# Half of a block's in-projection by Strassen products, with the weight sums made on the spot

## The chip, the cores and the metric

The kernel runs on one core of a Trainium2 chip. The metric is the time of one execution on the device in microseconds (us), lower is better. The engines of the core are PE (TensorE, matmuls), DVE (VectorE), ACT (ScalarE), POOL (GpSimd) and SP (SyncE). In this kernel SP issues the loads and POOL the stores; ACT and DVE evict, convert and add.

## What is computed

The reference is a trunk of two layers over 2048 tokens of width 1024. Per layer:

```python
shift, scale, gate = split(silu(c) @ w_ada[l] + b_ada[l])
h = rms_norm(x, g_pre[l]) * (1 + scale) + shift
u_a, b_a, c_a, gate_a, u_p, gate_p = split(h @ w_in[l])      # 6 x 512 columns
y_a = b_a * causal_conv3(c_a * u_a, w_conv[l]) * silu(gate_a)
y_p = pool_windows(u_p, w_pool[l], pool_scale[l]) * silu(gate_p)
y = concat(y_a, y_p) @ w_out[l]
x = x + gate * rms_norm(y, g_post[l])
```

Everything is fp32. The two large products of a layer are the in-projection (1024 by 3072 weights) and the out-projection (1024 by 1024).

## The kernel before

**Tiling.** Tokens lie along the free dimension, features on the 128 partitions. The work falls into four blocks (l, b): layer 0 with tokens 0 to 1023 and 1024 to 2047, then layer 1 with the same; they are called blocks 0 to 3. A block is an in-projection and an out-projection. Each fp32 product is made from three passes in the reduced type fp32r: every operand is split into a high half (a cast by ACT, L209 and L739) and a low half (operand less high half, by DVE, L219 and L749), and the passes are high by high, high by low, low by high (`PASSES`). One matmul is 128x128 weights by 512 tokens.

**In-projections.** Blocks 0 and 1 use `in_phase`: 24 column groups (kinds ua, up, ca, gp, ba, ga; four of each), 8 steps of k, 3 passes, 2 halves of tokens, so 1152 matmuls in block 1. Blocks 2 and 3 use `in_seven`: the groups are taken in 12 pairs (`PAIRS`: P is up and gp, A is ua and ca, B is ba and ga), and each pair is computed by the seven products of Strassen's scheme in Winograd's form, 12 matmuls each: 1008 in all. The scheme needs four sums of the pair's weight quarters, S1 to S4, and four of the operand's, T1 to T4. The weight sums of layer 1 are made by background tasks in blocks 0 and 1 (`sum_task`), split, stored to DRAM (`sums`) and loaded by POOL in blocks 2 and 3 (L724). The operand sums are made in the out-projection before (`operands` in `out_phase`).

**Order.** The order of each engine is written out by hand: DVE, ACT, PE, POOL and SP each run the instructions in the order of the code. Work that follows a group (evictions, gate, windows, convolution) is queued and given out in small steps between the matmuls. `Paced` spreads background tasks evenly over the turns of an in-projection; a task has a load that is issued when the task before it starts, and steps. The tasks are: `finish_tasks` (fin: an out-projection's result times the norm ry, plus x, stored as the next x; L1095 to L1115), `ada_task` (products of the conditioning, L265), `mix_task` (small matmuls on the pool weights of layer 1, tiles wupt and ps_wu, L419) and `sum_task` (L462 to L479). In block 1 the tasks are eight mixes, 16 fins, 16 adas of two products each, and the sums of the P pairs; the others were made in block 0. Weights are loaded, and their halves made, two to three halves ahead of their use.

**Tiles.** `working(t, r, n, w, v)` sets the number of buffers of each ring: `tmp` (1024 tokens wide), `half` (512), `landing` (512, loads of background tasks), raw weights, and v. A ring hands its tiles out in turn; who takes a tile waits until the last user of that tile is done. Block 1 has working(8, 6, 4, 3, 0), and there a wide sum task takes one tile of `tmp` for its four inputs (raw01).

**Between the phases.** An out-projection is 8 groups of 48 matmuls, `OUT_ORDER` giving the order of k for the first group (k = 3 last). At the end of a Strassen block the last steps of y and the first out-projection weights are made by the functions of `closing`.

## Time and profile before

| | us |
|---|---|
| median of 3 runs | 1411.99 |
| least, greatest | 1409.59, 1415.24 |
| profiled execution | 1412.32 |
| its span in the trace | 1410.5 |
| PE busy | 1385.0 |
| DVE busy | 920.7 |
| ACT busy | 493.5 |
| block 1: in-projection, out-projection (PE) | 393.6 to 666.6, to 753.8 |
| blocks 2 and 3: in-projections (PE) | 753.8 to 984.2, 1071 to 1301.8 |

The profiled execution has its own time, and the span of its trace is a little shorter than that time, since it runs from the first to the last instruction. "Busy" adds up the durations of an engine's instructions. A row of the timeline merges equal instructions that follow each other.

### The profile page before, as it was taken

Reading aid. Unit: us, or ns where it says so; the run is one execution under the profiler, and the core shown is the slowest. Engines: PE = TensorE matmul, PEld = TensorE weight load, DVE = VectorE, ACT = ScalarE, POOL = GpSimd, SP = SyncE. Lnnn points to the kernel's source line nnn. Section 1 sums busy time; section 2 is a strip of 40 time slices with the busy share of each in tenths; the row PEclk is TensorE's granted clock in tenths of the full one; section 3 lists DMA queues with packets and bytes.
Section 4 is the critical chain, followed back from the end, with each engine's and each line's share of the span. In section 5 each row is a group of like instructions: output and inputs, shape, how many; then the busy total and the mean of one; then the engine's idle time right before and its main releaser. Section 6 shows DMA issues by size and latency. Waiting matters only on the chain.

```text
span 1410.5 us, 17844 instructions
## 1 busy us (share of the span) xinstructions
PE 1385.0 (98%) x6250; PEld 1140.9 (81%) x6250; DVE 920.7 (65%) x1540; ACT 493.5 (35%) x862; POOL 219.7 (16%) x350
## 2 busy tenths in 40 slices
PE   8999999999999999999999999999999999999996
PEld 4778888888887888888888888888887888888796
DVE  7764778754545585866766776768866665657455
ACT  5332334345443323233546122123646121113421
POOL 0001232311101111101112222110112222211000
PEclk9999999999999999999999999999999999999998
DMA  8506777734436655645559888888459777877422
GB/s 323 179 31 205 232 250 273 247 130 156 157 116 200 228 180 193 227 161 172 183 187 310 259 246 260 264 246 259 175 188 311 224 225 221 244 226 245 144 90 90
DMA packets 143115, 291.22 MB, mean 206 GB/s; under 512 B 15921, under 2 KB 32305, under 8 KB 143026
## 3 DMA queue, kind: packets, MB, share of 16 engines
q1 hardware_dynamic: 96338, 171.58, 37.4%
q0 software_dynamic: 46688, 118.51, 25.5%
q8 instruction: 49, 0.80, 0.2%
q14 instruction: 40, 0.33, 0.1%
HBM read 217.67 MB, written 72.35 MB: 206 GB/s over the span
## 4 chain that ended last, share of the span: by engine, by line
PE 93%; DMA 3%; DVE 2%; issue 1%; ACT 1%; POOL 0%; SPq 0%; ACTq 0%; DVEq 0%; POOLq 0%
PE ps_in L393 36%; PE ps_in L817 29%; PE ps_out L393 24%; PE ps_wu L419 1%; DMA ws<-sums 1%; DMA yt<-fin 1%; DMA wupt<-wupt 1%; PE ps_warm L1219 1%; PE ps_stat L1236 1%; PE ps_stat L311 0%; DMA raw<-wout 0%; DVE y L186 0%; PE ps_c L1283 0%; DVE win L495 0%; DMA yraw<-yin 0%
## 5 line engine op out<-in xcount | busy, mean ns | idle before, releaser
L817 PE MATMUL ps_in<-h,ws 128*128 128x512 f32 x2016 | 458.6, 389 | 0.7 <-DMA ws<-sums 0.7
L393 PE MATMUL ps_in<-h,ws 128*128 128x512 f32 x1968 | 450.6, 390 | 0.0
L817 PEld LDWEIGHTS ps_in<-h,ws 128*128 128x128 f32 x2016 | 378.1, 188 | 80.2 <-DMA ws<-sums 1.6
L393 PEld LDWEIGHTS ps_in<-h,ws 128*128 128x128 f32 x1968 | 368.5, 188 | 76.2
L393 PE MATMUL ps_out<-y,ws 128*128 128x512 f32 (+1 forms) x1728 | 354.8, 367 | 2.6 <-DVE y L186 2.6
L393 PEld LDWEIGHTS ps_out<-y,ws 128*128 128x128 f32 x1728 | 299.9, 189 | 56.9 <-DVE y L186 2.9
L209 ACT CAST ws<-raw 128x512 fp32r<-128x512 f32 x146 | 89.9, 622 | 301.3 <-PE ps_in L393 156.7
L219 DVE TENSOR_TENSOR ws<-raw,ws 128x512 fp32r<-128x512 f32 x146 | 99.8, 688 | 125.3 <-ACT ws L209 125.1
L724 POOL DMA_DIRECT2D ws<-sums x96 | 67.7, 706 | 205.5 <-PE ps_in L817 182.6
L393 PE MATMUL ps_in<-h,w 128*128 128x512 f32 x336 | 81.9, 402 | 5.2 <-DVE h L385 2.8
L393 PEld LDWEIGHTS ps_in<-h,w 128*128 128x128 f32 x336 | 63.6, 191 | 22.6 <-DVE h L385 3.6
L739 ACT CAST ws<-raw 128x512 fp32r<-128x512 f32 x72 | 43.2, 617 | 66.8 <-PE ps_in L817 37.0
L1004 POOL DMA_DIRECT2D ysp<-yg x48 | 26.2, 545 | 241.6 <-ACT yg L1003 241.4
L265 DVE SCALAR_TENSOR_TENSOR adaw<-adaw,cb 128x512 f32<-128x512 f32 x64 | 43.1, 686 | 11.3 <-DMA adaw<-wada 9.6
L749 DVE TENSOR_TENSOR ws<-raw,ws 128x512 fp32r<-128x512 f32 x72 | 49.3, 684 | 0.0
L1012 DVE TENSOR_TENSOR acc<-acc,sq 128x512 f32<-128x512 f32 x42 | 28.9, 692 | 27.0 <-ACT sq L1009 27.0
L859 ACT ACTIVATE second<-second 128x1024 f32<-128x1024 f32 x16 | 17.0, 1061 | 82.6 <-DVE second L853 79.8
L838 ACT COPY v<-ps_in 128x512 f32<-128x512 f32 x24 | 14.1, 588 | 84.7 <-PE ps_in L817 84.7
L476 POOL DMA_DIRECT2D sums<-s13h x24 | 17.7, 739 | 146.6 <-ACT s13h L468 97.7
L1099 DVE TENSOR_TENSOR fin<-fin,ry 128x512 f32<-128x512 f32 x48 | 32.9, 685 | 8.3 <-DMA fin<-ysp 8.3
L853 DVE TENSOR_TENSOR second<-ps_in,v 128x512 f32<-128x512 f32 x16 | 11.0, 690 | 41.3 <-PE ps_in L817 41.3
L1003 ACT ACTIVATE yg<-ps_out,gg 128x512 f32<-128x512 f32 x48 | 33.1, 689 | 11.9 <-PE ps_out L393 11.9
(172 smaller groups left out, 1258.4 us busy)
## 6 DMA issues: line engine op xcount, KB each, us to landing
ws<-sums POOLq DMA_DIRECT2D x96, 512.0 KB, 7.6
raw<-win SPq DMA_DIRECT2D x122, 256.0 KB, 4.6
adaw<-wada SPq DMA_DIRECT2D x64, 256.0 KB, 4.8
raw<-wout SPq DMA_DIRECT2D x64, 256.0 KB, 3.2
sums<-raw POOLq DMA_DIRECT2D x48, 256.0 KB, 5.4
ysp<-yg POOLq DMA_DIRECT2D x48, 256.0 KB, 3.7
fin<-ysp SPq DMA_DIRECT2D x48, 256.0 KB, 4.3
raw<-win SPq DMA_DIRECT2D x80, 128.0 KB, 4.7
```

Of the source, the lines that this page charges most:

```text
L209: nc.scalar.copy(self.ws[m][:, 0], self.raws[m].rearrange("p (a b) -> p a b", b=P))
L219: nc.vector.tensor_tensor(t[:, 1], raw, t[:, 0].bitcast(F32), op=ALU.subtract)
L265: nc.vector.scalar_tensor_tensor(w[n], w[n], 1.0, cb[:, n * HS : (n + 1) * HS], op0=ALU.mult, op1=ALU.mult, accum_out=m[:, l, j : j + 1])
L393: nc.tensor.matmul(ps[s], lhsT=ws[k // KH][:, wi, k % KH, :], rhs=rhs(k, ri, s), start=first and (wi, ri) == PASSES[0], stop=last and (wi, ...
L724: nc.gpsimd.dma_start(ops[m].rearrange("p a b c -> p a (b c)"), sums[l, n][:, :, SUM[a]])
L739: nc.scalar.copy(ops[m][:, 0], raws[m].rearrange("p (a b) -> p a b", b=P))
L749: nc.vector.tensor_tensor(ops[m][:, 1], raw, ops[m][:, 0].bitcast(F32), op=ALU.subtract)
L817: nc.tensor.matmul(ps, lhsT=ops[m][:, wi, k, :], rhs=h[hn][k][:, ri, :], start=p < 4 and k == 0 and (wi, ri) == (0, 0), stop=k == KH - 1 a ...
L1003: nc.scalar.activation(t, ps[s], AF.Copy, scale=gg[:, l, j : j + 1])
L1004: nc.gpsimd.dma_start(ysp[l, b][:, j, s * HS : (s + 1) * HS], t)
L1012: tt(accs[s], accs[s], q, op=ALU.add)
L1099: nc.vector.tensor_tensor(e[0], e[0], ry[l, b, s], op=ALU.mult)
```

## The change

In block 1 the groups with index below `PLAIN` = 2 (12 of 24) stay plain, and the other 12 are computed as six Strassen pairs. Their weight sums don't come from DRAM: the class `Sevenths` loads the four quarters of a pair, and `add` makes S1, S2, S3 (L758 to L760 of the changed kernel) and later S4 (L765) on DVE; all seven weight operands are then split into high (ACT) and low half (DVE, L787). The out-projection of block 0 makes plain operands and, of the same values, the four differences (`both_operands`); what the Strassen half needs later is stored to `late4` and loaded as 16 background tasks (`fills`) in the plain half. The products y of block 1 go to DRAM and back as in blocks 2 and 3. The 16 conditioning tasks of layer 1 move from block 1 into block 0. The sum tasks of block 1 become narrow (wide=False): they take two tiles of `landing` (raw0, raw1) in place of one of `tmp`; three run in the plain half and five in the Strassen half, with six and ten fins. Block 1 has working(5, 6, 5, 6, 2). Three background tasks are primed and not one. The last product's evictions in every Strassen block stand behind the last closing function, not ahead of it. Where helpers moved, the changed kernel's numbers are L476 for L474 (a sum task's low halves), L1180, L1181 and L1186 for L1095, L1096 and L1101 (a fin's two loads and its sum), L868 for L817 (Strassen's matmuls) and L897 and L901 for L844 and L848 (evictions).

```diff
+    late4 = dram.tile([P, KH, 2, TB], F32, name="late4")
...
         def put_y(k, t, o, n):
+            if some:
+                nc.gpsimd.dma_start(yin[l, b][:, k, o : o + n], t)
+                return
...
-        bg.prime(1)
+        bg.prime(3)
...
+    class Sevenths:
+
+        def __init__(self, l, ring, pairs, made=False):
+            self.l, self.ring, self.pairs, self.made = l, ring, pairs, made
...
+                elif q == 0:
+                    self.raws[m] = self.raws[m + 1] = self.quarter(n, 0, 0)
+                    self.raws[m + 2] = self.quarter(n, 1, 0)
+                    self.raws[m + 5] = self.quarter(n, 1, 1)
+                elif q == 4:
+                    self.raws[m] = self.raws[m + 2] = self.quarter(n, 0, 1)
+                self.loaded += 1
+        def add(self, m):
+            tt = nc.vector.tensor_tensor
+            if m % 7 == 1:
+                self.low(m)
+                r11, r21, r22 = self.raws[m], self.raws[m + 1], self.raws[m + 4]
+                s1 = self.raws[m + 2] = half("s1")
+                tt(s1, r21, r22, op=ALU.add)
+                tt(r21, r11, r21, op=ALU.subtract)
+                tt(r11, s1, r11, op=ALU.subtract)
+                self.s2 = r11
+                return 3 * E2
+            if m % 7 == 6:
+                self.low(m - 1)
+                tt(self.raws[m], self.raws[m], self.s2, op=ALU.subtract)
+                return E2
+            return 0
+        def high(self, upto):
+            self.load(upto)
+            us = 0
+            while self.highs < min(upto, self.nm):
+                m = self.highs
+                if m in self.raws:
+                    if self.made:
+                        us += self.add(m)
+                    nc.scalar.copy(self.place(m)[:, 0], self.raws[m].rearrange("p (a b) -> p a b", b=P))
+                self.highs += 1
+            return us
+        def low(self, upto):
+            us = 0
+            while self.settled < min(upto, self.nm):
+                m = self.settled
+                if m in self.raws:
+                    t, raw = self.ops[m], self.raws.pop(m).rearrange("p (a b) -> p a b", b=P)
+                    nc.vector.tensor_tensor(t[:, 1], raw, t[:, 0].bitcast(F32), op=ALU.subtract)
+                    us += E2
+                self.settled += 1
+            return us
+        def settle(self, upto):
+            return self.high(upto) + self.low(upto)
...
+                if final and p == 6:
+                    closing[p](kept)
...
-                if at == 6:
-                    closing[at](kept)
-                if (n or p > 5) and n < len(PAIRS) - 1 and at != -1:
+                if (n or p > 5 or not opening) and n < len(pairs) - 1 and at != -1:
...
+        def both_operands(k):
             xs = []
 
             def load():
-                xs.append(tmp("xin")[:, :TB])
-                nc.sync.dma_start(xs[0], x_src(nl, k, nb * TB, TB))
+                for kk in (k, k + KH):
+                    xs.append(tmp("xin")[:, :TB])
+                    nc.sync.dma_start(xs[-1], x_src(nl, kk, nb * TB, TB))
 
             def steps():
-                t = xs[0]
-                nc.vector.scalar_tensor_tensor(t, t, apre[:, nl, k : k + 1], rn, op0=ALU.mult, op1=ALU.mult)
-                yield E1
+                a, c = xs
+                for t, kk in ((a, k), (c, k + KH)):
+                    nc.vector.scalar_tensor_tensor(t, t, apre[:, nl, kk : kk + 1], rn, op0=ALU.mult, op1=ALU.mult)
+                    yield E1
                 yield None
                 parts = []
-                for s in range(NH):
-                    hp0[s][k] = slot(next(hp), [P, 2, HS], "h")
-                    u = t[:, s * HS : (s + 1) * HS]
-                    parts.append((hp0[s][k], u))
-                    nc.scalar.activation(hp0[s][k][:, 0], u, AF.Identity, bias=mod[:, nl, k : k + 1])
+                for t, kk in ((a, k), (c, k + KH)):
+                    nc.scalar.activation(t, t, AF.Identity, bias=mod[:, nl, kk : kk + 1])
+                    for s in range(NH):
+                        d = hp0[s][kk] = slot(hplaces[8 * s + kk], [P, 2, HS], "h")
+                        u = t[:, s * HS : (s + 1) * HS]
+                        nc.scalar.copy(d[:, 0], u)
+                        parts.append((d, u))
                 yield None
                 for d, u in parts:
-                    prenorm_lo(d[:, 0], d[:, 1], nl, k, u)
+                    tt(d[:, 1], u, d[:, 0].bitcast(F32), op=ALU.subtract)
                     yield E2
+                a0, a1, c0, c1 = [u for _, u in parts]
+                for dst, p, m in ((a0, a1, a0), (a1, c1, a1), (c1, c1, a0), (c0, c0, c1)):
+                    tt(dst, p, m, op=ALU.subtract)
+                    yield E2
+                nc.gpsimd.dma_start(spill4[:, k, 0], a)
+                nc.gpsimd.dma_start(spill4[:, k, 1], c)
...
+                if both and j == KT - 1 and n == 6:
+                    nxt.high(3)
+                    nxt.settle(2)
+                if not both and j == KT - 1 and n == 4:
+                    nxt.load(2)
...
+            rest += [ada_task(1, j) for j in list(range(8, 16)) + list(range(8))]
+            rest += [call_task(lambda: (ada_fin(1, 1, 0, KT), ada_fin(1, 0, 0, KT)), 0.5)]
...
+    with working(5, 6, 5, 6, 2), tc.manual_schedule():
+        plain = [(kind, i) for kind, i in IN_ORDER if i < PLAIN]
+        pairs = [(kind, i) for kind, i in PAIRS if i >= PLAIN]
+        first = in_weights(0, plain, 0, turned(ws.places, 16))
+        h, fills, opening, hrhs = out_phase(0, 0, y, 0, 1, ws, hplaces, yorder, first, True)
+        ring = first.places + hplaces[8 : 8 + KH]
+        wts = Sevenths(0, ring, pairs, True)
         later = Later()
         mixes = [mix_task(1, g, n, later) for g in range(NCG) for n in range(2)]
         fins = finish_tasks(0, 0, later)
-        adas = [ada_task(1, j) for j in list(range(8, 16)) + list(range(8))]
-        adas += [call_task(lambda: (ada_fin(1, 1, 0, KT), ada_fin(1, 0, 0, KT)), 0.5)]
-        sums_ = [sum_task(1, n, u, True) for n, u in mine("P")]
-        tasks = between(mixes, fins[:4]) + between(between(adas, sums_), fins[4:])
-        ws = out_weights(0, first.places)
-        y = in_phase(0, 1, hrhs, tasks, later, None, yplaces, first.places, ws, first, opening)
-    wplaces = first.places
+        sums_ = [sum_task(1, n, u, False) for n, u in mine("P")]
+        cut = 6
+        tasks = between(fills, mixes) + between(fins[:cut], sums_[:3])
+        in_phase(0, 1, hrhs, tasks, later, None, None, first.places, wts, first, opening, plain)
+        hp = {}
+        for k in range(KH):
+            hp["B11", k], hp["B21", k], hp["B22", k] = hplaces[k], hplaces[KH + k], hplaces[12 + k]
+        it = iter(yorder)
+        for name in ("T2", "T3", "T1", "T4"):
+            for k in range(KH):
+                hp[name, k] = next(it)
+        ws, closing, done = block_end(0, 1, hp, ring, pairs, False, (3, 2, 3, 2, 2, 2))
+        kept = in_seven(0, 1, h, [], None, between(fins[cut:], sums_[3:]), later, wts, closing, pairs)
+        y, yorder, wplaces, hplaces, _ = done(kept)
```

**PE, in-projection of block 1.** ps_in are the sums of the in-projection, ps_wu those of a mix, ps_stat a mean of squares. Before, and changed:

```order
L419 MATMUL ps_wu<-wp,wupt 128x128 x4
L393 MATMUL ps_in<-h,ws 128x512 x366
L311 MATMUL ps_stat<-ah,ones 128x512
L311 MATMUL ps_stat<-al,ones 128x512
L393 MATMUL ps_in<-h,ws 128x512 x558
```

```order
L421 MATMUL ps_wu<-wp,wupt 128x128 x4
L395 MATMUL ps_in<-h,ws 128x512 x318
L868 MATMUL ps_in<-h,ws 128x512 x156
L313 MATMUL ps_stat<-ah,ones 128x512
L313 MATMUL ps_stat<-al,ones 128x512
L868 MATMUL ps_in<-h,ws 128x512 x312
```

Where 366 and 558 plain matmuls stood behind the last mix, 318 plain ones stand and then 468 of Strassen products (L868), around the first small statistics.

**DVE, second half of block 1's in-projection, at the end of a sum task.** s13 and s13h are a sum task's S1 and S3, raw01 or raw0 and raw1 its quarters, ws a weight's two halves, fin a finish task's tiles, ps_in an eviction. Before, and changed:

```order
L472 TENSOR_TENSOR s13_4870<-s13_4870,s13h_4871 128x512
L474 TENSOR_TENSOR raw01_4817<-raw01_4817 128x256 x2
L219 TENSOR_TENSOR ws_4941<-raw_4855,ws_4941 128x512
L604 TENSOR_TENSOR cv_4674<-cv_4674,sga_4945 128x1024
L265 SCALAR_TENSOR_TENSOR adaw_4898,mod_76<-adaw_4898,cb_70 128x512
L551 TENSOR_TENSOR y_4962<-cv_4674,y_4962 128x512
L551 TENSOR_TENSOR y_4964<-cv_4674,y_4964 128x512
L265 SCALAR_TENSOR_TENSOR adaw_4900,mod2_77<-adaw_4900,cb_70 128x512
L265 SCALAR_TENSOR_TENSOR adaw_4967,mod_76<-adaw_4967,cb_70 128x512
L219 TENSOR_TENSOR ws_4986<-raw_4896,ws_4986 128x512
L1115 TENSOR_TENSOR xacc_4450<-xacc_4450,fin_4866 128x512
L265 SCALAR_TENSOR_TENSOR adaw_4969,mod2_77<-adaw_4969,cb_70 128x512
```

```order
L474 TENSOR_TENSOR s13_4868<-s13_4868,s13h_4869 128x512
L476 TENSOR_TENSOR raw0_4812<-raw0_4812 128x256
L476 TENSOR_TENSOR raw1_4815<-raw1_4815 128x256
L787 TENSOR_TENSOR ws_4964<-raw_4841,ws_4964 128x512
L901 TENSOR_TENSOR second_4895<-ps_in_4974,second_4895 128x512
L1184 TENSOR_TENSOR fin_4916<-fin_4916,ry_3532 128x512
L1186 TENSOR_TENSOR fin_4917<-fin_4917,fin_4916 128x512
L787 TENSOR_TENSOR ws_4988<-raw_4921,ws_4988 128x512
L758 TENSOR_TENSOR s1_5013<-raw_4923,raw_4925 128x512
L759 TENSOR_TENSOR raw_4923<-raw_4921,raw_4923 128x512
L760 TENSOR_TENSOR raw_4921<-s1_5013,raw_4921 128x512
L1200 TENSOR_TENSOR xacc_4811<-xacc_4811,fin_4864 128x512
```

Before, a sum task's last low halves are followed by a weight's low half, the gate product and conditioning products, with the next fin eleven rows behind; now a fin's two steps stand three and four rows behind, then the low half and the sums of the next pair's weights.

**SP, the loads of the same stretch.** Each row is one load in the order of SP's queue; wu is the mixed pool weight, ysp the out-projection's stored result. Before, and changed:

```order
L200 DMA raw_4813<-win 128x512
L454 DMA raw01_4817<-win 128x256
L454 DMA raw01_4817<-wu1_2_94 128x256
L454 DMA raw01_4817<-win 128x256
L454 DMA raw01_4817<-wu1_2_94 128x256
L200 DMA raw_4855<-wu0_3_91 128x512
L1095 DMA fin_4866<-ysp0_0_130 128x512
L1096 DMA fin_4867<-xt 128x512
L200 DMA raw_4896<-wu0_3_91 128x512
L261 DMA adaw_4898<-wada 128x512
L261 DMA adaw_4900<-wada 128x512
L200 DMA raw_4943<-win 128x512
```

```order
L456 DMA raw0_4812<-win 128x256
L456 DMA raw0_4812<-wu1_2_94 128x256
L456 DMA raw1_4815<-win 128x256
L456 DMA raw1_4815<-wu1_2_94 128x256
L729 DMA raw_4841<-win 128x512
L1180 DMA fin_4864<-ysp0_0_131 128x512
L1181 DMA fin_4865<-xt 128x512
L1180 DMA fin_4916<-ysp0_0_131 128x512
L1181 DMA fin_4917<-xt 128x512
L729 DMA raw_4921<-wu0_3_91 128x512
L729 DMA raw_4923<-win 128x512
L729 DMA raw_4925<-win 128x512
```

Before, a sum task takes one tile of `tmp` (raw01) and the fin takes two of `landing`; now raw0, raw1 and four fin tiles are taken one after the other from `landing`, and the three quarters of the next pair stand behind the last of them.

## Rows read from the trace of the kernel before

**Rows 1.** Chain that ended last, by engine and line, share of the span.

```profile
PE 93%; DMA 3%; DVE 2%; issue 1%; ACT 1%; POOL 0%; SPq 0%; ACTq 0%; DVEq 0%; POOLq 0%
PE ps_in L393 36%; PE ps_in L817 29%; PE ps_out L393 24%; PE ps_wu L419 1%; DMA ws<-sums 1%; DMA yt<-fin 1%; DMA wupt<-wupt 1%; PE ps_warm L1219 1%; PE ps_stat L1236 1%; PE ps_stat L311 0%; DMA raw<-wout 0%; DVE y L186 0%; PE ps_c L1283 0%; DVE win L495 0%; DMA yraw<-yin 0%
```

**Rows 2.** What PE waited for, whole span: us in total, times, longest us.

```profile
PE ps_wu L419 <- DMA wupt<-wupt: 3.6, 2, 2.3
PE ps_out L393 <- DVE y L186: 2.6, 1, 2.6
```

**Rows 3.** Timeline of PE, merged: start us, us, line, operation, tiles, count.

```profile
535.47 126.70 PE L393 MATMUL ps_in<-h,ws 128*128 128x512 f32 x558
666.61 87.20 PE L393 MATMUL ps_out<-y,ws 128*128 128x512 f32 x384
765.57 117.17 PE L817 MATMUL ps_in<-h,ws 128*128 128x512 f32 x516
```

**Rows 4.** Stretches, length, busy us of PE, PEld, DVE, ACT, POOL; granted clock, DMA.

```profile
113.00:306.60 193.60, 192.35 (x873) 159.92 (x871) 133.28 (x264) 71.23 (x142) 48.80 (x70) 1.00 0.70 237
306.60:393.60 87.00, 87.00 (x385) 72.07 (x384) 45.96 (x61) 42.02 (x71) 7.60 (x14) 1.00 0.43 148
393.60:535.60 142.00, 139.67 (x648) 116.44 (x648) 82.58 (x148) 47.49 (x85) 18.32 (x30) 1.00 0.59 190
535.60:666.80 131.20, 131.20 (x580) 108.55 (x579) 87.33 (x162) 38.20 (x73) 19.05 (x28) 1.00 0.57 188
1310.00:1315.00 5.00, 5.00 (x16) 3.91 (x17) 2.38 (x4) 3.32 (x6) 0.00 (x0) 0.66 0.38 114
```

**Rows 5.** Timeline of DVE in block 2, and at the last in-projection's end.

```profile
797.13 1.28 DVE L514 SCALAR_TENSOR_TENSOR cv<-z,vecs,cv 128x1024 f32<-128x1024 f32 x1
798.33 0.69 DVE L1101 TENSOR_TENSOR fin<-fin 128x512 f32<-128x512 f32 x1
...
1306.45 0.68 DVE L873 TENSOR_TENSOR v<-ps_in,v 128x512 f32<-128x512 f32 x1
1307.17 0.69 DVE L773 TENSOR_TENSOR cv<-v,cv 128x512 f32<-128x512 f32 x1
1307.90 0.69 DVE L776 TENSOR_TENSOR cv<-cv,second 128x512 f32<-128x512 f32 x1
1308.51 0.69 DVE L219 TENSOR_TENSOR ws<-raw,ws 128x512 fp32r<-128x512 f32 x1
1309.11 1.29 DVE L186 TENSOR_TENSOR y<-cv,y 128x512 fp32r<-128x512 f32 x2
```

**Rows 6.** Lines by form, block 1's in-projection: busy us, mean ns.

```profile
L219 DVE TENSOR_TENSOR ws<-raw,ws 128x512 fp32r<-128x512 f32 x48 | 33.0, 687 | 38.5 <-ACT ws L209 38.5
L209 ACT CAST ws<-raw 128x512 fp32r<-128x512 f32 x48 | 29.9, 623 | 157.2 <-PE ps_in L393 99.7 <-issue 51.6 <-DMA raw<-wu 4.1
...
L474 DVE TENSOR_TENSOR raw<-raw 128x256 fp32r<-128x256 f32 x16 | 6.0, 417 | 0.0
L477 POOL DMA_DIRECT2D sums<-s x8 | 5.8, 728 | 15.4 <-DVE s L472 13.1 <-DMA fin<-ysp 2.1
L510 DVE TENSOR_SCALAR cv<-z,vecs 128x1024 f32<-128x1024 f32 x4 | 3.0, 748 | 0.0
```

**Rows 7.** DMA issues, second half of block 1, then first: us to landing.

```profile
sums<-raw POOLq DMA_DIRECT2D x10, 256.0 KB, 4.4
fin<-ysp SPq DMA_DIRECT2D x7, 256.0 KB, 3.3
fin<-xt SPq DMA_DIRECT2D x7, 256.0 KB, 4.1
sums<-s13h POOLq DMA_DIRECT2D x5, 256.0 KB, 2.7
...
sums<-raw POOLq DMA_DIRECT2D x6, 256.0 KB, 5.6
```

**Rows 8.** SP's waits in block 2's in-projection: us, times, longest.

```profile
SPq L1095 <- DMA x<-fin: 30.3, 5, 8.9
```

More of the change, by code (lines that the diff above doesn't have):

```diff
@@ L627, in in_phase @@
         else:
-            order, first = IN_ORDER, 0
+            order, first = some or IN_ORDER, 0
         for part in (range(0, 3), range(3, first)) if started else ():
@@ L673, in in_phase @@
                 turn = KT * (n - first) + k
+                if n == len(order) - 1 and k == 2:
+                    nxt.load(1)
                 if n == len(order) - 1 and k > KH:
@@ L704, in trunk, with place, quarter, load @@
     LOAD, HIGH, SETTLE = 6, 4, 3
-    def in_seven(l, b, h, fills, opening, tasks, later, ring, closing):
-        ops, raws = {}, {}
+    class Sevenths:
+        def __init__(self, l, ring, pairs, made=False):
+            self.l, self.ring, self.pairs, self.made = l, ring, pairs, made
+            self.ops, self.raws = {}, {}
+            self.nm = 7 * len(pairs)
+            self.loaded = self.highs = self.settled = 0
+        def place(self, m):
+            self.ops[m] = slot(self.ring[m % len(self.ring)], [P, 2, KH, P], "ws")
+            return self.ops[m]
+        def quarter(self, n, row, part):
+            kind, i = self.pairs[n]
+            t = held["w"].tile([P, HS], F32, tag="w", name="raw")
+            nc.sync.dma_start(t.rearrange("p (a b) -> p a b", b=P), w_src(self.l, PAIR_OF[kind][row], i, part))
+            return t
+        def load(self, upto):
+            while self.loaded < min(upto, self.nm):
+                m = self.loaded
+                n, q = divmod(m, 7)
+                a = PRODUCTS[q][0]
+                if a in SUM and not self.made:
+                    kind, i = self.pairs[n]
+                    t = self.place(m)
+                    nc.gpsimd.dma_start(t.rearrange("p a b c -> p a (b c)"), sums[self.l, PAIRS.index((kind, i))][:, :, SUM[a]])
+                elif not self.made:
+                    self.raws[m] = self.quarter(n, *QUARTER[a])
+                elif q == 0:
[44 more added lines that the diff above has]
+            return self.high(upto) + self.low(upto)
@@ L712, in in_seven @@
+    def in_seven(l, b, h, fills, opening, tasks, later, wts, closing, pairs):
         kept = {}
         ct = {}
-        nm = 7 * len(PAIRS)
-        pos = {"load": 0, "high": 0, "settle": 0}
-        def load(upto):
-            while pos["load"] < min(upto, nm):
-                m = pos["load"]
-                n, (a, _) = m // 7, PRODUCTS[m % 7]
-                kind, i = PAIRS[n]
-                if a in SUM:
-                    ops[m] = slot(ring[m % len(ring)], [P, 2, KH, P], "ws")
-                    nc.gpsimd.dma_start(ops[m].rearrange("p a b c -> p a (b c)"), sums[l, n][:, :, SUM[a]])
-                else:
-                    row, part = QUARTER[a]
-                    raws[m] = held["w"].tile([P, HS], F32, tag="w", name="raw")
-                    nc.sync.dma_start(
-                        raws[m].rearrange("p (a b) -> p a b", b=P), w_src(l, PAIR_OF[kind][row], i, part)
-                    )
-                pos["load"] += 1
@@ L754, in put_y @@
+        load, high, settle, ops = wts.load, wts.high, wts.settle, wts.ops
         def put_y(k, t):
@@ L1022, in out_phase @@
         work.q.append(norm())
-        ops = [plain_operands(k) for k in range(KT)] if plain else [operands(k) for k in range(KH)]
+        ops = [(both_operands if both else operands)(k) for k in range(KH)]
         ops[0][0]()
@@ L1047, in out_phase, with fill @@
         spare = {}
-        if plain:
-            plain.settle(3)
-        def fill(n, name, k, it=iter(lplaces or [])):
+        if both:
+            nxt.settle(3)
+        it = iter(lplaces)
+        def fill(name, k, src):
             p = next(it)
@@ L1060, in fin, with steps @@
                 settle(t, spare.pop((name, k)))
-            return load, fin
-        fills = [] if plain else [fill(n, name, k) for n, name in enumerate(LATE) for k in range(KH)]
+            def steps():
+                t = h[name][k] = slot(p, [P, 2, HS], "h")
+                raw = spare.pop((name, k))
+                nc.scalar.copy(t[:, 0], raw)
+                yield None
+                tt(t[:, 1], raw, t[:, 0].bitcast(F32), op=ALU.subtract)
+                yield E2
+            return (load, steps, E2) if both else (load, fin)
+        if both:
+            cut = {"T1": (0, 0), "T3": (0, HS), "T4": (1, 0), "T2": (1, HS)}
+            fills = [
+                fill(name, k, spill4[:, k, cut[name][0], cut[name][1] : cut[name][1] + HS])
+                for name in ("T2", "T3", "T1", "T4") for k in range(KH)
+            ]
+        else:
+            fills = [fill(name, k, spill[:, k, n]) for n, name in enumerate(LATE) for k in range(KH)]
         st = {}
```

128 lines of the change are left out of this document (55 added, 73 removed).

## Prediction

> **What bounds the kernel now.** I read the chain of waits first: 93% of the path that ends last is PE, and the largest part is the in-projection's matmul line [rows 1]. The waits say how little PE loses: 3.6 us for the pool weights of layer two (tile wupt) and 2.6 us for the low half of the last y [rows 2]. So a matmul that is taken out of PE's row is worth its whole duration, as long as PE is still fed. The timeline gives that price: 558 matmuls in 126.70 us are 0.227 us each, and 516 in a Strassen block take 117.17, the same; an out-projection of 384 takes 87.20, which is 1.36 for one k step of six [rows 3]. The busy times by stretch say who could take PE's place: in block 1's in-projection, the place of the change, DVE works 82.58 of 142.00 and then 87.33 of 131.20 us and in block 0's 133.28 of 193.60 [rows 4]. DVE is second, and the change gives it work.
>
> A busy DVE microsecond is not one of DVE's pace. An instruction of 0.69 us lets the next start after 0.60 where that doesn't read it and after 0.73 where it does; 1024 columns take 1.28 and let the next start after 1.20 [rows 5]. So I count a step as the duration less 0.085, and 0.125 more behind an instruction that it reads.
>
> The Trainium skill ("VectorE: DVE Perf Modes", section "The TRN2 errata — SBUF-src ops pay a fixed extra latency per instruction") gives an fp32 tensor_tensor (N+151)/0.96 ns, 691 at 512 columns, which agrees with the 688 of [rows 6]. Taken as the price of each instruction in a row, it would make DVE's own lateness, worked out as 10 us further down, 26, and the time some 1440, inside the last rival; the starts in [rows 5] stand against that.
>
> **The change part by part.** The base is the profiled execution of 1412.3 us; the median of the runs lies 0.3 lower, so no correction is made.
>
> Matmuls of block 1: 1152 before; now 12 plain groups of 48 are 576 and 42 products of 12 are 504. 72 are gone: 72 × 0.2267 = **−16.3**.
>
> Waits for wupt: three background loads are primed and not one, and in block 1 fills stand between the mix tasks, so their loads have more turns to land. The 3.6 goes: **−3.6**, at least 0.
>
> Last transition: the low halves of y's last pair now come ahead of the two evictions and the product with second. Before, from L873's start at 1306.45 to L219's at 1308.51 there were 2.1 us of them ahead of the two halves that PE waited 2.6 for [rows 2, 5]: **−2.1**, between 0 and −2.6. In the five microseconds after that wait the granted clock was 0.66, between the levels of 1.2 and 2.4 GHz, with 16 matmuls where 22 fit (5 ÷ 0.227), so up to 1.4 more may come back [rows 4]; I take none.
>
> Block 0 gets 16 condition tasks, 32 products of 128x512 at 0.60 to 0.69, 19 to 22 us of DVE in a stretch in which it idled for 60 [rows 4, 6]. Cost **0**, up to 2 where tasks bunch. Out-projection of block 0: the new operand differences are some 10 us more on DVE, which was busy 45.96 of 87.00 us [rows 4]: 0. Plain half of block 1: its tasks are 70 to 76 us of DVE steps beside 131 us of PE for the 576 matmuls alone: 0, up to 2.
>
> *Strassen half of block 1, DVE.* From the last plain group's gate product to the last low half of y, DVE has 213 instructions: 156 of 512 columns, 30 of 256, 19 of 1024 and more, and 8 tiny. By steps: 156 × 0.603 = 94.1 and 30 × 0.335 = 10.0 [rows 6]; of the 19, 17 at 1.20 [rows 5] and two of the 748 ns kind at 0.67 [rows 6], together 21.7; tiny 0.7. 33 of them read the one ahead: 33 × 0.125 = 4.1. Sum 130.6. It starts late by about 1.5 us, an estimate: it waits for two silu on ACT, each like a copy of 0.62 [rows 6]. And a low half L787 (changed kernel) stands behind the sum L760 or L765 that its high half is copied from, 0.62 of ACT and two handovers [rows 6]: some eight times 0.4 to 1.0, together about 3. DVE needs **135**. PE has 42 × 12 × 0.2267 = 114.3, with two small statistics 115; y's last pair is read at the eighth k step of the out-projection, 7 × 1.36 = 9.5 later. So PE allows 125 and comes **10** late, the look-ahead of three products being in these numbers.
>
> *Strassen half, transfers.* The sum tasks are narrow now: they and the finish tasks (fin) draw on one ring `landing`, with five tiles for block 1. In the row on SP in the section on the change the takers are raw0, raw1, fin_4864, fin_4865, fin_4916 and fin_4917: the sixth gets raw0's tile back. It can be loaded only when DVE has made raw0's low part (L476), POOL has issued the store, behind that of s13 (0.73 an issue [rows 6]; half a microsecond of that left), the store has landed (4.4), and the load behind it has (4.1) [rows 7]. That is 9.0 us, and DVE's row has the consumer (L1186, fin_4917) only four instructions behind L476, 2.1 us by steps. DVE stands still for 6.9. Four finish loads stand so, 9, 4, 7 and 2 instructions behind (5.8, 2.1, 4.0 and 0.9 us): waits of 3.3, 6.9, 5.1 and 8.1, **23.4**. SP issues in order, so the next pair's three quarter loads stand behind the waiting one; the low half right behind it comes 0.6 late in three cases: **1.8**. Once more, early in the half, a sum task's load waits for a store of x by a finish task, with its consumer ten instructions (6.1 us) behind, by the same 9.0: **2.9**. Together 28 us, and with the 10 of DVE's own row 38. Before, the same queue waited for such stores too, 30.3 us in five cases in block 2, without harm, since there the tasks stand long before their use [rows 8].
>
> Bounds: with the stretch's quick transfers of the same size, 2.7 for the store and 3.3 for the load, the four waits are 13.5 and the lateness 28; with the 5.6 that the same store took in the first half, 44 [rows 7]. I take 35, nearer to the medians of the very transfers (38) than to either end.
>
> What the Trainium skill ("DMA: Bandwidth & Descriptors", section "Anatomy of one DMA — SWDGE (gpsimd) path") gives for such a store is 2.0 us plus bytes over 436e3, an estimate of 2.6 for 256 KB, against 4.4 in the row. By 2.6 for both transfers the lateness would be 22 and the change worth nothing, which is the rival of quick transfers further down; the rows are of this stretch, so they decide.
>
> Sum: 1412.3 − 16.3 − 3.6 − 2.1 + 35 = **1425**.
>
> **The rivals.** *DVE's row alone is late.* The landing loads aren't late, because the tiles come free earlier than I read or DVE reaches the sums sooner; then 10 us remain: 1412.3 − 22 + 10 = 1400. This is the other side, faster. It decides at a lateness of 22, which is a store and a load of 5.4 us together where the rows say 8.5. For it: [rows 8], a queue that waits without harm. Against it: two instructions of cover.
> *DVE has slack.* If steps of a half with few PE waits run together better, or the row I count is covered by the look-ahead altogether, all gains stay: 1412.3 − 22 = 1390. For it: nothing in PE's waits of a Strassen block names DVE. Against it: the sums L758 to L765 and three more low halves a pair stand in no row of before.
> *Quick transfers.* If the four stores land like the quickest of their kind and the loads too, 2.7 each, 5.4 together, the four waits fall to some 10 and the lateness to 22 to 23: 1412.3 − 22 + 22.5 = 1413, no change. For it: the row of 2.7 is of the same stretch and size; against it: it is one store of four of a task, and these are the third ones [rows 7].
> *Transfers slower, clock lower.* With 5.6 for store and 4.1 for load, and a quarter of PE's gaps followed by a stretch like 1310 to 1315, 1412.3 − 22 + 44 + some 5 to 10 = 1440 to 1445.
> That the change doesn't do what it says is excluded by PE's row: 318, 156 and 312 matmuls stand where 366 and 558 stood.
>
> **How the numbers follow.** The forecast, 1425 (1416 to 1436), gets 0.60; DVE's row alone, 1400 (1394 to 1405), 0.16; DVE with slack, 1390 (1386 to 1394), 0.10; slower still, 1437 to 1450, 0.08; quick transfers, 1413 (1405 to 1416), 0.06. The range leaves out the two outer cases: 1394 to 1436. The measurement of this kernel can tell about 0.5%, 7 us, from no change. Faster than 1405: 0.16 + 0.10 = 0.26. Within 7 us, up to 1419: 0.06 and a tenth of the forecast, 0.12. Slower: 0.62.
>
> **What would show it.** In the changed kernel's trace: no PE wait for wupt; 0.227 us a matmul in the Strassen half between gaps; PE waiting there for low halves by L787, 25 us or more in all; DVE waiting at L1186 for the load of x, four times, 3 to 8 us; SP waiting at L1181 for the store of the sums; the wait ahead of the last out-projection about half a microsecond. Wrong would be: DVE's waits at L1186 small (the rival of 1400), DVE idle in that half and PE never waiting (1390), or a loss outside of block 1's in-projection.

## The result and the profile after

| | median us | least, greatest |
|---|---|---|
| before | 1411.4 | 1409.6, 1415.2 |
| changed kernel | 1435.4 | 1431.7, 1437.2 |

The ratio is 1.0163 (95% interval 1.0134 to 1.0193): slower by 23 us, though 72 matmuls are gone. The forecast was 1425 (1416 to 1436), so the time lies at that case's upper end. The profiled execution took 1435.3 us, its span is 1433.5.

Where the time went is read off the places at which PE changes its phase. These lines of the changed kernel's timeline of PE (start, duration, line, tiles, count, and in brackets the idle time ahead and what ended it) answer to [rows 3]:

```profile
311.00 87.20 PE L395 MATMUL ps_out<-y,ws 128*128 128x512 f32 x384
398.04 13.77 PE L395 MATMUL ps_in<-h,ws 128*128 128x512 f32 x60
...
464.79 72.36 PE L395 MATMUL ps_in<-h,ws 128*128 128x512 f32 x318
536.99 35.53 PE L868 MATMUL ps_in<-h,ws 128*128 128x512 f32 x156
...
606.31 10.61 PE L868 MATMUL ps_in<-h,ws 128*128 128x512 f32 x38 [5.30 <-ACT ws L777]
...
659.42 13.73 PE L868 MATMUL ps_in<-h,ws 128*128 128x512 f32 x50 [8.04 <-ACT fin L1197]
...
687.71 10.32 PE L395 MATMUL ps_out<-y,ws 128*128 128x512 f32 x43 [0.88 <-ACT ws L211]
...
778.27 11.22 PE L868 MATMUL ps_in<-h,ws 128*128 128x512 f32 x48
...
1325.82 1.51 PE L395 MATMUL ps_out<-y,ws 128*128 128x512 f32 x5
```

The plain half is clean (318 matmuls in 72.36 us are 0.2275 each). The Strassen half begins at 536.99 and reaches the out-projection only at 687.71, 150.7 us for 115 of matmuls. By phase, before and changed:

| phase | before | changed | difference |
|---|---|---|---|
| block 0, to its out-projection | 306.6 | 311.0 | +4.4 |
| its out-projection | 87.0 | 87.0 | 0.0 |
| in-projection of block 1 | 273.0 | 289.7 | +16.7 |
| its out-projection | 87.0 | 90.6 | +3.5 |
| blocks 2 and 3 to the last out-projection | 548.2 | 547.6 | −0.6 |
| last out-projection to the end | 108.7 | 107.7 | −1.0 |

The busy times of the two halves of block 1 (columns as in [rows 4]):

```profile
398.00:537.00 139.00, 139.00 (x646) 116.04 (x646) 75.64 (x121) 50.44 (x92) 18.82 (x31) 1.00 0.56 188
537.00:687.00 150.00, 125.70 (x509) 95.89 (x507) 120.41 (x196) 46.78 (x88) 21.80 (x34) 0.95 0.50 166
```

In the first half DVE is busy for 75.64 of 139 us. In the second PE is idle for 24 us, DVE is busy for 120.41 of 150, and the granted clock is 0.95 on average, between 1.2 and 2.4 GHz: it is 0.83 from 600 to 610 and 0.69 from 650 to 660, around PE's two longest gaps, and 0.93 from 660 to 687. What DVE waited for from 530 to 700 (us in all, times, longest), then SP's queue, then DVE's four waits one by one:

```profile
DVE fin L1186 <- DMA fin<-xt: 18.7, 4, 6.8
DVE ws L787 <- ACT ws L777: 7.1, 7, 2.4
DVE cv L609 <- ACT sga L607: 4.9, 1, 4.9
DVE ws L221 <- ACT ws L211: 2.2, 1, 2.2
DVE y L188 <- ACT y L185: 1.3, 2, 0.7
```

```profile
SPq L1181 <- DMA sums<-raw: 47.4, 4, 14.6
```

```profile
574.22 0.69 DVE L1186 TENSOR_TENSOR fin<-fin 128x512 f32<-128x512 f32 x1 [2.64 <-DMA fin<-xt]
...
605.04 0.69 DVE L1186 TENSOR_TENSOR fin<-fin 128x512 f32<-128x512 f32 x1 [6.80 <-DMA fin<-xt]
...
628.33 0.69 DVE L1186 TENSOR_TENSOR fin<-fin 128x512 f32<-128x512 f32 x1 [3.12 <-DMA fin<-xt]
...
657.38 0.69 DVE L1186 TENSOR_TENSOR fin<-fin 128x512 f32<-128x512 f32 x1 [6.14 <-DMA fin<-xt]
```

The longest of the seven waits at L787, 2.4, and the one at L609 end before 538.1, where DVE's row of the Strassen half begins.

SP's queue stands four times at L1181, the fin's second load, for the store of a sum task's tile, and each time DVE stands at the addition that reads the load. PE names ACT's weight copies (L777) or whatever came last in ACT's or DVE's row as its releaser, but these stand behind the waiting addition: the next pair's sums are made after it, and ACT's copies are of these sums. One of the four, the second, followed through the timelines of DVE, POOL and SP:

```profile
595.68 0.75 DVE L476 TENSOR_TENSOR raw<-raw 128x256 fp32r<-128x256 f32 x2
...
598.50 0.67 POOL L481 DMA_DIRECT2D sums<-raw  x1 [1.71 <-DVE fin L1184]
...
601.27 0.33 SPq L1181 DMA_DIRECT2D fin<-xt  x1
601.65 0.42 SPq L729 DMA_DIRECT2D raw<-wu  x1
```

The first of the two L476 makes raw0's low part, by its start and its duration of 0.42 until 596.1. POOL issues the store at 598.50, it has landed when SP issues the load at 601.27, 2.8 us later, and DVE goes on at 605.04, 3.8 us after that: 8.9 us in all, where the forecast had 9.0. The next pair's quarter load (L729) comes right behind on SP.

Block 0 lost its 4.4 us at its last statistics. Before, they ran without a gap; in the changed kernel PE waits, and the 30 matmuls behind them take 8.29 us and not 6.99. PE before, PE in the changed kernel, and one of ACT's waits there:

```profile
299.31 0.40 PE L311 MATMUL ps_stat<-ah,ones 128*128 128x512 f32 x1
...
299.77 6.99 PE L393 MATMUL ps_in<-h,ws 128*128 128x512 f32 x30
```

```profile
301.55 0.51 PE L313 MATMUL ps_stat<-ah,ones 128*128 128x512 f32 x1 [3.27 <-ACT ah L368]
...
302.87 8.29 PE L395 MATMUL ps_in<-h,ws 128*128 128x512 f32 x30
```

```profile
ACT ah L368 <- DMA sums<-s13h: 3.8, 1, 3.8
```

ah is the high half of the last sum of squares, and ACT could write its tile of the ring `half` only when the store of a sum task's s13h had been read out of it.

### The profile page after: what moved, and what is told of

It is laid out like the page before. It is cut to its first block, busy times and chain, and to the rows that moved or that the text cites. A ratio compares the mean times of both kernels' runs of the same rounds, so it can differ in the third digit from the quotient of the medians.

```text
span 1433.5 us, 17996 instructions
## 1 busy us (share of the span) xinstructions
PE 1379.6 (96%) x6178; PEld 1126.0 (79%) x6178; DVE 982.8 (69%) x1645; ACT 522.6 (36%) x905; POOL 227.0 (16%) x365
## 4 chain that ended last, share of the span: by engine, by line
PE 73%; issue 9%; DVE 9%; DMA 5%; ACT 2%; POOL 1%; SPq 1%; DVEq 0%; ACTq 0%; POOLq 0%
PE ps_in L868 31%; PE ps_out L395 23%; PE ps_in L395 17%; DMA raw<-win 1%; PE ps_wu L421 1%; DMA sums<-raw 1%; DMA raw<-wout 1%; DVE y L188 1%; DVE ws L221 1%; DVE win L497 1%; DMA fin<-xt 0%; PE ps_warm L1304 0%; DVE adaw L267 0%; PE ps_stat L1321 0%; DMA xin<-xt 0%
## 5 line engine op out<-in xcount | busy, mean ns | idle before, releaser
L868 PE MATMUL ps_in<-h,ws 128*128 128x512 f32 x2520 | 583.8, 392 | 24.1 <-ACT ws L777 13.2
L868 PEld LDWEIGHTS ps_in<-h,ws 128*128 128x128 f32 x2520 | 473.5, 189 | 133.0 <-ACT ws L777 16.9
L395 PEld LDWEIGHTS ps_in<-h,ws 128*128 128x128 f32 x1392 | 261.4, 189 | 54.1
L211 ACT CAST ws<-raw 128x512 fp32r<-128x512 f32 x122 | 74.7, 621 | 192.2 <-PE ps_in L395 73.0
L221 DVE TENSOR_TENSOR ws<-raw,ws 128x512 fp32r<-128x512 f32 x122 | 83.2, 687 | 83.2 <-ACT ws L211 83.2
L777 ACT CAST ws<-raw 128x512 fp32r<-128x512 f32 x108 | 65.3, 618 | 170.7 <-DMA raw<-win 49.0
L787 DVE TENSOR_TENSOR ws<-raw,ws 128x512 fp32r<-128x512 f32 x108 | 73.9, 685 | 7.3 <-ACT ws L777 7.1
L912 ACT ACTIVATE second<-second 128x1024 f32<-128x1024 f32 x20 | 21.2, 1062 | 85.5 <-DVE second L906 82.6
L891 ACT COPY v<-ps_in 128x512 f32<-128x512 f32 x30 | 17.6, 585 | 83.2 <-PE ps_in L868 83.2
L1186 DVE TENSOR_TENSOR fin<-fin 128x512 f32<-128x512 f32 x48 | 32.9, 685 | 20.1 <-DMA fin<-xt 20.0
```

Source lines behind the costliest of these rows:

```text
L211: nc.scalar.copy(self.ws[m][:, 0], self.raws[m].rearrange("p (a b) -> p a b", b=P))
L221: nc.vector.tensor_tensor(t[:, 1], raw, t[:, 0].bitcast(F32), op=ALU.subtract)
L395: nc.tensor.matmul(ps[s], lhsT=ws[k // KH][:, wi, k % KH, :], rhs=rhs(k, ri, s), start=first and (wi, ri) == PASSES[0], stop=last and (wi, ...
L777: nc.scalar.copy(self.place(m)[:, 0], self.raws[m].rearrange("p (a b) -> p a b", b=P))
L787: nc.vector.tensor_tensor(t[:, 1], raw, t[:, 0].bitcast(F32), op=ALU.subtract)
L868: nc.tensor.matmul(ps, lhsT=ops[m][:, wi, k, :], rhs=h[hn][k][:, ri, :], start=p < 4 and k == 0 and (wi, ri) == (0, 0), stop=k == KH - 1 a ...
```

## Experiments

The theory after the trace: the Strassen half is late because DVE's row there is longer than PE allows, and because landing tiles go from a sum task to a fin a few instructions later (the chain of tiles). Rival A: DVE's row alone, its waits at L1186 standing where it would wait anyway. Rival B: the chain alone. A third reading, C: the weight sums made on the spot are late in themselves.

**Fins first** (e1): order changed, no work.

```diff
-        kept = in_seven(0, 1, h, [], None, between(fins[cut:], sums_[3:]), later, wts, closing, pairs)
+        kept = in_seven(0, 1, h, [], None, fins[cut:] + sums_[3:], later, wts, closing, pairs)
```

> In the Strassen half all ten fins stand ahead of the five sum tasks; no work is added or left out. Theory (two causes: the landing tiles' chain from a sum task's store to the next fin's load, and DVE's own row): DVE's four waits at L1186 (18.7 us in all) go, and with them some 5 us of late weight halves; DVE's own lateness of 10 to 14 stays: about 1411, against 1435. Rival A (DVE's row alone sets the pace, the waits at L1186 only stand where DVE would wait anyway): 1433 to 1437. Rival B (the chain is the only cause): about 1397.

1426.9 us, ratio 1.0106 (1.0088 to 1.0124). Between the readings. The trace says why: the waits at L1186 are gone, but the sum tasks, now one behind the other, wait for each other's stores in the same ring (DVE's waits, then SP's):

```profile
DVE s L464 <- DMA raw<-win: 9.5, 3, 5.8
```

```profile
SPq L456 <- DMA sums<-raw: 22.8, 4, 10.3
SPq L1181 <- DMA x<-fin: 22.0, 3, 11.9
```

So an order alone moves the chain to another task; this neither confirms 1411 nor excludes B.

**Seven tiles** (e2): the order of the changed kernel.

```diff
-    with working(5, 6, 5, 6, 2), tc.manual_schedule():
+    with working(5, 6, 7, 4, 2), tc.manual_schedule():
```

> Order as in the changed kernel; the ring of landing tiles has 7 and not 5, paid for with two raw weight tiles (4 and not 6). Theory: the fin that follows a sum task gets a tile freed a task earlier, the waits at L1186 fall under 5 us in all: 1411 to 1416, up to 1422 if four raw tiles make the quarters late. Rival A: 1433 or more. Rival B: about 1397.

1414.1 us, ratio 1.0017 (1.0005 to 1.0030), 21 us less than the changed kernel. DVE doesn't wait at L1186 any more (one wait for a sum's load remains, `L464`, 1.9 us). The Strassen half takes 130.2 us and not 150.7:

```profile
538.50:668.70 130.20, 120.56 (x510) 95.46 (x509) 121.22 (x199) 48.75 (x92) 21.78 (x34) 0.99 0.60 201
```

DVE's work is the same 121 us, now in 130. Rival A, which left no gain, falls. 15 us over PE's 115 remain, so B falls too.

**Seven tiles and a shorter row of DVE** (e5). The diff against e2:

```diff
-        while w < WINDOWS[g]:
+        while w < (2 if short else WINDOWS[g]):
...
         yield 0.7 * n / TB
+        if short:
+            return
...
-            pd = yield from windows(l, b, i, u)
+            pd = yield from windows(l, b, i, u, wts.made)
...
-            yield from conv(l, i, ct[i], z, 0, TB)
+            yield from conv(l, i, ct[i], z, 0, TB, wts.made)
```

> As e2 (7 landing tiles, 4 raw tiles), and in the Strassen half of block 1 DVE's later window additions (5) and the second and third steps of the convolution (4) are left out, so its output differs: 10.6 us of DVE steps less, nothing else. Theory (what is left in e2 is DVE's own row): about 1404, against 1414. Rival (what is left is something else: late raw quarters, ACT's copies, the lower clock after gaps): 1411 or more.

1406.6 us, ratio 0.9966 (0.9953 to 0.9980): 7.5 us less than e2 for 10.6 us of steps. DVE's row does set the pace of what remains, for the most part; seven tenths came back. Why not all isn't shown; the nine instructions lie in a few places, and where DVE is no longer behind, a saving brings PE nothing.

**All tasks in the plain half** (e3), five tiles:

```diff
-        tasks = between(fills, mixes) + between(fins[:cut], sums_[:3])
+        tasks = between(fills, mixes) + between(fins, sums_)
...
-        kept = in_seven(0, 1, h, [], None, between(fins[cut:], sums_[3:]), later, wts, closing, pairs)
+        kept = in_seven(0, 1, h, [], None, [], later, wts, closing, pairs)
```

> All 16 fins and 8 sum tasks stand in the plain half; the Strassen half has no background task. Some 32 us of DVE steps move to a half in which DVE was busy 76 of 139 us. Theory: DVE's row in the Strassen half is about 98 us against 115 of PE, the chain's waits fall on a DVE with slack: no lateness left, 1397, up to 1402. A third reading (C: the sums and halves of the weights themselves come too late, by ACT's copies behind DVE's sums): 10 us or more of PE's waits for L777 and L787 stay, 1408 or more.

1452.2 us, ratio 1.0290 (1.0274 to 1.0306): 50 us over the top of the expectation, yet the Strassen half did what it should. Busy times of the two halves, and DVE's waits in the first:

```profile
398.60:590.00 191.40, 154.09 (x639) 123.90 (x638) 109.27 (x187) 63.54 (x118) 38.77 (x61) 0.89 0.63 210
590.00:706.60 116.60, 116.60 (x516) 96.56 (x515) 89.37 (x133) 36.47 (x65) 2.16 (x4) 1.00 0.28 92
```

```profile
DVE fin L1186 <- DMA fin<-xt: 30.8, 9, 7.3
DVE s L464 <- DMA raw<-win: 14.6, 7, 4.4
...
DVE fin L1184 <- DMA fin<-ysp: 8.2, 7, 2.4
```

Without background tasks PE runs 116.60 of 116.60 us in Strassen products, at the full clock, with all sums made on the spot: reading C falls. The chain of five tiles went with the tasks: DVE waited 54 us for landing loads in the plain half and stopped PE in its turn (29.3 us of PE's waits name L221, the weights' low halves), and the granted clock was 0.89 there, between 1.2 and 2.4 GHz. What the expectation left out is that DVE's spare time hides nothing when the waits stand in its own row.

**Seven tiles, tasks moved** (e6 and e7). Both have working(5, 6, 7, 4, 2) and, in block 0, the order of e4. e7 has e3's tasks, e6 five fins and two sums moved:

```diff
-        cut = 6
-        tasks = between(fills, mixes) + between(fins[:cut], sums_[:3])
+        cut = 11
+        tasks = between(fills, mixes) + between(fins[:cut], sums_[:5])
...
-        kept = in_seven(0, 1, h, [], None, between(fins[cut:], sums_[3:]), later, wts, closing, pairs)
+        kept = in_seven(0, 1, h, [], None, between(fins[cut:], sums_[5:]), later, wts, closing, pairs)
```

> 7 landing tiles and 4 raw tiles, the statistics early as in e4, and 5 fins and 2 sum tasks more in the plain half (11 and 5 there, 5 and 3 in the Strassen half): 15 us of DVE steps moved. Theory: DVE's row in the Strassen half is 116 us against 125 that PE allows, the chain is one task longer in both halves: 1435 - 38 - 4 + up to 6 of remaining waits = 1393 to 1400. Rival (the plain half's chain now stalls DVE and PE as in e3): 1405 to 1415.

> As e6, with all 16 fins and 8 sum tasks in the plain half, none in the Strassen half. Theory (e3's loss of 53 us was the chain of five tiles in the plain half, where DVE waited 54 us for landing loads): with seven tiles most of these waits go; 1395 to 1405. Rival (in e3 the plain half's loss is DVE's load or the pacing, not the tiles): 1430 or more.

e6: **1396.0 us**, ratio 0.9887 (0.9866 to 0.9909), faster than both kernels. Block 1's in-projection is full of PE work in both halves:

```profile
395.70:534.00 138.30, 138.30 (x642) 115.46 (x642) 90.25 (x150) 56.45 (x103) 27.36 (x44) 1.00 0.70 238
534.00:649.70 115.70, 115.70 (x511) 95.75 (x511) 106.27 (x170) 43.41 (x80) 13.44 (x21) 1.00 0.48 167
```

That is 254.0 us from 395.7 to 649.7, where 273.0 less the 16.3 of the matmuls and 2.3 of one wait for wupt is 254.4: the gain that the change holds is all there once DVE isn't late. e7: 1414.8 us, ratio 1.0021 (1.0009 to 1.0033). Two tiles more, with some 3 us of e4's order, took 37 us off e3, so the tiles were most of e3's loss; but DVE still waited in the plain half (7.9 us at L464 for loads, 6.0 at L1184) and the time is 19 us longer than e6's. Its expectation was too low; by these waits seven tiles aren't enough for 24 tasks in one half.

**Four tiles** (e8): the chain drawn tighter, working(5, 6, 4, 6, 2).

> The changed kernel with 4 landing tiles and not 5, nothing else. Theory (the chain of tiles): a taker now waits for the one four places ahead, so each fin that follows a sum task waits for a later store, and a sum task for the store of x by the fin just ahead: DVE's waits for landing loads in the Strassen half grow from 19 to 35 us or more, the time to 1450 or more. Rival A (DVE's row alone): 1433 to 1438.

1450.4 us, ratio 1.0274 (1.0237 to 1.0310), 15 us more than the changed kernel. The waits for landing loads grew from 18.7 to 31.4 us, somewhat less than expected, and moved to the fin's first load as well:

```profile
DVE fin L1184 <- DMA fin<-ysp: 18.5, 4, 6.8
DVE fin L1186 <- DMA fin<-xt: 9.7, 5, 3.7
...
DVE s L464 <- DMA raw<-win: 3.2, 5, 1.1
```

With 4, 5 and 7 tiles the times are 1450, 1435 and 1414: the ring's length is a cause, and rival A is out for good.

**Block 0: statistics early** (e4), and **the tasks alone** (e9). e4 is the changed kernel with

```diff
+            rest += [x_stat_task(1, s, k, accs) for s in range(NH) for k in range(KT)]
+            rest += [x_stat_end(1, s, accs, later) for s in range(NH)]
             rest += [ada_task(1, j) for j in list(range(8, 16)) + list(range(8))]
             rest += [call_task(lambda: (ada_fin(1, 1, 0, KT), ada_fin(1, 0, 0, KT)), 0.5)]
-            rest += [x_stat_task(1, s, k, accs) for s in range(NH) for k in range(KT)]
...
-            tasks += [x_stat_end(1, s, accs, later) for s in range(NH)]
```

and e9 the kernel before with the 16 conditioning tasks moved:

```diff
+            rest += [ada_task(1, j) for j in list(range(8, 16)) + list(range(8))]
+            rest += [call_task(lambda: (ada_fin(1, 1, 0, KT), ada_fin(1, 0, 0, KT)), 0.5)]
...
-        tasks = between(mixes, fins[:4]) + between(between(adas, sums_), fins[4:])
+        tasks = between(mixes, fins[:4]) + between(fins[4:], sums_)
```

> In block 0 the 16 tasks of sums of squares and the two that end them stand ahead of the 16 conditioning tasks of layer two, and not behind; nothing else. Theory (the changed kernel's 4.4 us in block 0 are the last statistics' operand that comes late behind the bunched tasks): the waits of PE at L313 (3.9) go, 1431. Rival (DVE is overloaded in block 0 as a whole): no change, 1435.

> The kernel before with one part of the change: the 16 conditioning tasks of layer two stand in block 0 and not in block 1. Theory (the tasks push the last statistics of block 0 behind the end of its column groups): PE waits some 4 us for the statistics near the end of block 0, 1414 to 1417 against 1412. Rival (the 4.4 us come from the out-projection's new operands or elsewhere): 1411 to 1412.

e4: 1432.2 us, ratio 1.0146 (1.0131 to 1.0161), 3 us less than the changed kernel; block 0's out-projection begins at 307.90 and not 311.00. The last statistics stand at 221 to 226 us, with one wait of 1.6 in place of the 3.9. Counted from block 0's first matmul of split weights to its out-projection, 192.9 us before became 197.8 in the changed kernel and 193.3 in e4. e9: 1416.3 us, ratio 1.0032 (1.0015 to 1.0049), 4.2 more than the 1412.2 beside it, with the same wait in the kernel of before:

```profile
305.30 0.49 PE L311 MATMUL ps_stat<-ah,ones 128*128 128x512 f32 x1 [3.48 <-ACT ah L366]
306.03 0.80 PE L311 MATMUL ps_stat<-al,ones 128*128 128x512 f32 x1 [0.23 <-DVE al L368]
```

So the wait of block 0 comes with the moved tasks: the same matmul, the same releaser, the same length, and ACT waits 4.0 us for a store of s13h here too. That the time's 4.2 meets the 4.4 is chance: in e9's trace block 0 ends 8.1 us later than before (314.67 against 306.60) and the rest is 5.3 shorter. DVE wasn't full (151.89 of 193.00 us busy in e9): 16 more tasks ahead put the statistics, which stood last in the list, behind a store of the sum tasks that shares their ring.

**The last closing function** (e10): e6 with the old order of the last evictions.

```diff
-                if final and p == 6:
-                    closing[p](kept)
...
                 free = mix.run(free)
+                if at == 6:
+                    closing[at](kept)
```

> e6 with the evictions of a Strassen block's last product put back ahead of the last closing function. Theory (the new order trades one wait of 2.6 for three of 2.1 in all at the last out-projection, since ACT's copy of the next weight moves behind the last half of y): the single wait of 2.6 comes back there, 1396 to 1398. Rival (the order matters more, 2 us at each of two blocks): 1399 to 1401.

1399.9 us, ratio 0.9909 (0.9880 to 0.9938); its runs (1394.6 to 1401.3) and those of e6 (1393.3 to 1399.5) overlap, so the times decide nothing, though the median lies where the rival had it. The traces do for one place: the single wait came back, 2.62 us for y's low half, and the last out-projection to the end takes 107.3 us against 107.7 in e6. That part of the change is worth nothing that can be seen.

## Why the prediction held, and where its steps did not

By the spans the change cost 23.0 us, where the forecast's sum has 13. Of the 10 between them 5.7 are block 0, 3.8 the Strassen half with the out-projection behind it, 1.1 the last transition, and blocks 2 and 3 give 0.6 back. So the direction and the mechanism held, and the range held by 0.6 us. One of the forecast's own signs of being wrong came true beside that: 4.4 and 3.5 us were lost outside of block 1's in-projection.

**The matmuls**, −16.3: right. e6 has them as a gain, to 0.4 us.

**wupt**, −3.6: right. PE has no wait for it in the changed kernel. The reasons given are only in part shown: in e9, without the other primed loads and the fills, block 0's wait is there (2.0 us), but that of block 1, 2.3 before, is gone; and e3, which has both, has one of 2.0.

**The last transition**, −2.1: the phase shrank by 1.0, and e10 shows that the order isn't what did it. The step counted what moved ahead (y's first low half) and not what moved behind. These are ACT and DVE of the changed kernel there; they answer to the end of [rows 5]:

```profile
1334.56 0.62 ACT L185 CAST y<-cv 128x512 fp32r<-128x512 f32 x1 [3.20 <-DVE cv L827]
1335.20 1.28 ACT L944 ACT_TABLE_LOAD   x1
1336.49 0.62 ACT L211 CAST ws<-raw 128x512 fp32r<-128x512 f32 x1
...
1335.21 0.69 DVE L188 TENSOR_TENSOR y<-cv,y 128x512 fp32r<-128x512 f32 x1 [0.74 <-ACT y L185]
1337.14 0.69 DVE L221 TENSOR_TENSOR ws<-raw,ws 128x512 fp32r<-128x512 f32 x1 [1.24 <-ACT ws L211]
```

Before, both halves of y came in one go at 1309.11, 7.3 and 7.9 us behind the out-projection's first matmul at 1301.81. Now that matmul is at 1325.82, the first half 5.9 us behind it (1331.73), but the second (1335.21) 9.4, since it needs the evictions and the product that were moved behind the first; the next weight's copy (1336.49) follows it. One wait of 2.6 became three, 0.3, 0.6 and 1.2, where the forecast had half a microsecond left. None of its rivals has a wait that takes another's place.

**Block 0**, 0 to 2: measured 4.4. It should have gained 1.25, the wait for wupt that stood in it before and went, so it is 5.7 over the forecast. The step that failed is that some 20 us more of DVE's steps cost nothing in a stretch in which it idled for 60. The room was there in DVE's sum, but the sum doesn't decide: what counts is what stands last in the list of tasks and who waits for it. It is the largest miss.

**The Strassen half**, 35: measured 38.8 (16.7 + 3.5 of the two phases, and the 18.6 that the matmuls and one wait for wupt had taken off). The two causes are right by e2, e5 and e8, and by e3 and e6, which take both away. DVE's whole row came out as forecast: 135 and 28 make 163 us from the end of the plain groups to y's last low half, and from 536.99 to that instruction's end at 699.71 are 162.7. Its terms, however, are off in both directions:

- DVE's steps: 130.6 forecast. From L609's start at 538.08 to 699.71 are 161.6 us, with 28.8 us of waits in them: 132.8 over the 213 instructions, 2.2 more.
- The four waits at L1186: 3.3, 6.9, 5.1 and 8.1 forecast, 2.6, 6.8, 3.1 and 6.1 measured, 18.7 for 23.4. From the end of L476 to the fin were 8.4, 8.9, 7.1 and 7.1 us, not 9.0 each.
- The parts of these came out otherwise. POOL issued the store 0.7, 2.4, 0.7 and 0.7 us behind L476 (0.5 forecast), SP the load 2.8 us after that in all four (4.4), and DVE went on 5.0, 3.8, 3.6 and 3.6 us later (4.1). The stores and loads of the three other cases:

```profile
566.52 1.41 POOL L481 DMA_DIRECT2D sums<-raw  x2
621.95 1.41 POOL L481 DMA_DIRECT2D sums<-raw  x2
650.99 1.41 POOL L481 DMA_DIRECT2D sums<-raw  x2
...
569.27 0.33 SPq L1181 DMA_DIRECT2D fin<-xt  x1
624.70 0.33 SPq L1181 DMA_DIRECT2D fin<-xt  x1
653.75 0.33 SPq L1181 DMA_DIRECT2D fin<-xt  x1
```

- The stores' median in this half is 2.7 us. The Trainium skill ("DMA: Bandwidth & Descriptors", section "Anatomy of one DMA — SWDGE (gpsimd) path"), whose estimate of 2.6 for such a store was set aside for the row's 4.4, agrees with that. The rival of quick transfers still did not come true, since the loads were not as quick as the stores. The forecast's lower bound of 28, which takes such transfers, should have been about 26 by its own rule, since the sum task's 2.9 shrinks with them too.
- The sum task's load, 2.9: DVE did not wait there. SP's queue did stand for the store of x, 3.7 us at L456, but the load went out at 547.12 and its consumer, L464, began at 549.27 without a wait.
- Low halves that come late by ACT's copies and the quarter loads, 3 and 1.8 forecast: 4.6 at L787 within the row. (Eight times 0.4 to 1.0 are 3.2 to 8, so the 3 was the low end.)
- Other waits, none forecast: 5.5 in all, of them 2.2 at the out-projection's first weights and 1.3 at y.
- The out-projection after block 1: 3.5 us, of which some 2 are no lateness of DVE. In e6, without any stall before it, it still has a wait of 1.05 us for a weight's low half and takes 89.3 (649.7 to 739.0). This was not forecast.

So that 38.8 lies near 35, and the row at 163, is partly luck: the chain took 7.6 less than forecast, the steps and the other waits 7.7 more. e2 says the same: with the chain away 17 us stayed (15 in the half, 2 in the out-projection), where the forecast had 10 for DVE's row alone.

**What the runs leave open.** Why POOL issued one of the four stores 2.4 us behind DVE and the others after 0.7; the profile names a DVE instruction that POOL doesn't need. e7's remaining 19 us were read off DVE's waits, not taken apart by a run. And whether more tiles of `half` would have saved block 0's statistics as well as their place in the list: e4 and e9 change the list alone.

## What to carry to other kernels

A task moved into an engine's idle time costs nothing only if nobody waits for what it pushes back; look at what stands last in the list, and at the tiles that its operands share with stores. Where loads of several background tasks share one ring, count for each taker how many instructions lie between the last use of its tile and its own first use; if that is less than a store and a load with their issues (7.1 to 8.9 us here), the consumer's engine stands still, busy share or not; two more tiles were worth 21 us here, more than the 16 of the matmuls saved. Spread work between phases by the row of the second engine in each (130 us of steps against 125 here), and test a layout by taking the tasks away altogether: PE at 116.60 of 116.60 us showed at once that the Strassen half itself was sound.

## What was not expected of the hardware

A store by POOL of 256 KB landed in 4.4 us (median) in the kernel before and in 2.7 in the same task's place in the changed kernel, with a DMA share of 0.57 before and 0.50 after: a median taken in one stretch isn't a price for another. And DVE kept nearly one pace over 213 mixed instructions, 132.8 us without their waits against 130.6 summed from a handful of starts.
